# Queries, keys and output gate of a hybrid encoder block as twelve pairs of seven part products

## The chip, the core and the metric

The kernel runs on one core of one Trainium2 chip. The metric is device time in microseconds (us). Three runs of the kernel before gave a median of 2877.66 us (2876.84 to 2880.89).

Five engines work side by side, each in its own program order and held up only by semaphores: TensorE (PE, with its weight loads shown as PEld), VectorE (DVE), ScalarE (ACT), GpSimd (POOL) and SyncE (SP), whose queue issues the DMAs.

## The reference

One encoder block over 2048 tokens of width 1024, in float32:

```python
xn = rms_norm(h, ln_mix_g);  proj = xn @ w_in            # 1024 -> 2512 columns
y_a = mlstm_group(proj q, k, v, o, gates, conv, norm_g)  # 4 heads x 128, both directions
y_b = mla_group(proj c_q, c_kv, k_rope, ...)             # 4 heads, latent queries, keys, values
h = h + concat(y_a, y_b) @ w_out
h = h + conv_gated_mlp(rms_norm(h), w_up, conv, w_down)
h = h + sigmoid(rms_norm(h) @ w_gate) * rms_norm(p @ w_proj)
out = rms_norm(h, final_g)
```

The change concerns `proj` and what follows it directly. Its 2512 columns are queries (512), keys (512), values (512), output gate (512) and a rest of 464 (16 gates, 256 query latents, 128 key-value latents, 64 rotary key columns). Queries and keys go through a depthwise convolution of width 3 along the tokens and a SiLU. Values are used as they are. The output gate goes through a sigmoid and multiplies the normed mLSTM output. The query latents are normed, multiplied by `w_uq`, and 64 columns of every head are rotated.

## The kernel before, in words

**Precision.** Each float32 operand is split into a high and a low part (`split`, L116: ACT casts the high part, DVE subtracts; `split_g`, L125, also multiplies by a gain). A product is three matmuls (`mm3`, L131): low by high, high by low, high by high.

**Stages.** `run` (L150) calls `in_proj`, then `attend` with the mLSTM as a side generator, then `stream`. PSUM has eight banks. During `in_proj` and `attend` they are four of pool `sc` and four of pools `tr`, `pv`, `ml`; during `stream` they are `fx`, `fy`, `fz`, `fs`, two each.

**in_proj (L176).** All of x is split once into sixteen SBUF places `x0` to `x15` and stays there. Three loops over the 16 token tiles follow, each with its weights resident: the rest (`rest`, L253, with the transposes of `turn_rest`, L283, two tiles later), the values (L330 to L338), the output gate (L340 to L348). One tile of one loop is `nat` (L212): 8 blocks of 128 inputs by 3 matmuls. The mLSTM gate arithmetic (`gates`, L641, a generator) is advanced once per tile in the second and third loop. Then queries and keys are computed transposed, channels on partitions: for each of 8 blocks of 128 channels, 4 blocks of 512 tokens, 24 matmuls each (`block`, L385), followed by convolution and SiLU (`taps`, `silu`). Within these blocks a second generator, `side`, is advanced every second input block: `absorb` (L528, it multiplies latent matrices into each other) and `q_up` (L573, the latent queries with their rotation). The last two blocks of channel block 7 stand in the attention.

**attend (L981).** For 64 pairs of head and query tile: scores, exponentials, transposes, the product with the latent values. The mLSTM (`mlstm`, L750) is advanced beside it at a rate set by the constant `SIDE`.

**stream (from L1535).** Output projection, MLP and the last gate. Here a product of 2 by 2 blocks is made from seven part products instead of eight (Strassen's scheme in Winograd's form). A *pair* is two output blocks of 128 by two blocks of 512 tokens; its seven products are called by `prod`, L1472, 12 matmuls each: A11 B11, S1 T1, S2 T2, A12 B21, S3 T3, A22 T4, S4 B22. The last two of a pair run inside the next pair. S1 to S4 are sums of weight blocks, T1 to T4 sums of the other operand. `sum4` (L1231) makes such sums, writes them to DRAM, and `split_op` (L1322) brings them back and splits them into the `x` places.

**Order.** A planner orders the instructions of each engine from their program order and its own estimate of times; in `manual_schedule` blocks the named engine keeps the written order. All DMAs of these stages are issued on SP's queue.

## Time and profile before

| | |
|---|---|
| median of the runs | 2877.66 us |
| profiled execution, its own time | 2877.3 us |
| its span, first to last instruction | 2875.3 us |
| PE busy | 2844.8 us, 99% |
| DVE busy | 2040.0 us, 71% |
| ACT busy | 1503.9 us, 52% |
| POOL busy | 216.6 us, 8% |
| moved by DMA | 508.93 MB, mean 177 GB/s |
| rest loop, value loop, output gate loop | from 7.6 us to 281.9 us of the span |
| queries and keys | from 281.9 us to 492.3 us |
| attention with mLSTM | from 492.3 us to about 1206 us |
| output projection, MLP, last gate | from about 1218 us to the end |

The page's first part gives each engine's busy time, its second the span in 40 slices. A "window" row gives the busy time of each engine between two points of the span with the number of instructions, the clock granted to PE, the share of the DMA engines and GB/s. A "group" row gives line, engine, operation, output and inputs, shape, count, then busy us, mean ns of one, and the idle time before them with what ended it. A "timeline" row gives start, length, engine, line and count of instructions in a row. Matmuls overlap in their pipeline, so that the length of one is more than the distance to the next; distances are read from the starts.

### The profile page before, as it was taken

The numbers are of one execution on the slowest core, as the hardware profiler recorded it, in microseconds if no ns is written. First come the engines' busy times: TensorE is split into PE (matmuls) and PEld (weight loads), VectorE is DVE, ScalarE is ACT, GpSimd is POOL, SyncE is SP. The second block draws the span as 40 slices with busy tenths as digits, with TensorE's granted clock in tenths as the row PEclk, the third lists the DMA queues.
The fourth block names the chain that finished last, engine by engine and source line by source line (L and its number), as shares of the span: only waits on it lengthen the run. The fifth ranks groups of instructions, "written<-read, shape, count | busy, mean of one in ns | idle before, by whom it ended". The sixth has DMA issues, their size and how long they took to land.

```text
span 2875.3 us, 40181 instructions
## 1 busy us (share of the span) xinstructions
PE 2844.8 (99%) x14110; PEld 2389.0 (83%) x14110; DVE 2040.0 (71%) x3726; ACT 1503.9 (52%) x3006; POOL 216.6 (8%) x331
## 2 busy tenths in 40 slices
PE   8999999999999999999999999999999999999998
PEld 7888888888888888888888888888888788888787
DVE  7521565777777777877778877877778767676787
ACT  7311544656666666755655555655556333254665
POOL 3100000000000100034200000000000000011012
PEclk9999999999999999999999999999999999999999
DMA  6612545464443333478845544657776757576864
GB/s 190 133 59 75 165 119 172 126 188 130 132 133 109 102 115 109 142 240 270 273 136 183 192 166 161 208 180 237 237 236 200 239 193 245 167 264 203 283 202 163
DMA packets 408313, 508.93 MB, mean 177 GB/s; under 512 B 34080, under 2 KB 271664, under 8 KB 408112
## 3 DMA queue, kind: packets, MB, share of 16 engines
q1 hardware_dynamic: 408112, 506.37, 55.4%
q8 instruction: 111, 1.82, 0.2%
q14 instruction: 90, 0.74, 0.1%
HBM read 324.16 MB, written 182.12 MB: 176 GB/s over the span
## 4 chain that ended last, share of the span: by engine, by line
PE 51%; DMA 3%; DVE 3%; ACT 1%; issue 1%; POOL 0%; SPq 0%; POOLq 0%; ACTq 0%; DVEq 0%
PE fy L1472 20%; PE fz L1472 14%; PE fx L1472 13%; PE fs L133 1%; DMA opr<-tw_d 1%; DMA opr<-t_d 1%; DVE op L123 1%; DVE fw L123 0%; ACT op L120 0%; DVE fgv L1520 0%; PE fs L1770 0%; PE fs L1894 0%; PE tb L997 0%; PE ppv L1009 0%; ACT fw L120 0%
## 5 line engine op out<-in xcount | busy, mean ns | idle before, releaser
L1472 PE MATMUL fz<-op,fw 128*128 128x512 f32 x1968 | 479.9, 392 | 5.1 <-ACT fw L120 4.8
L1472 PE MATMUL fx<-op,fw 128*128 128x512 f32 x1968 | 475.8, 390 | 0.0
L1472 PE MATMUL fy<-op,fw 128*128 128x512 f32 x1968 | 474.6, 390 | 0.0
L1472 PEld LDWEIGHTS fz<-op,fw 128*128 128x128 f32 x1968 | 368.1, 188 | 84.2 <-ACT fw L120 6.4
L1472 PEld LDWEIGHTS fy<-op,fw 128*128 128x128 f32 x1968 | 368.6, 188 | 76.4
L1472 PEld LDWEIGHTS fx<-op,fw 128*128 128x128 f32 x1968 | 368.1, 188 | 76.0
L120 ACT CAST pt<-tb 128x512 fp32r<-128x512 f32 x256 | 147.4, 586 | 179.9 <-PE tb L997 178.8
L1472 PE MATMUL fy<-op,fwd 128*128 128x512 f32 (+1 forms) x984 | 238.0, 390 | 0.6 <-DVE uv L1457 0.6
L133 PE MATMUL bk<-wsp,xh 128*128 128x512 f32 (+1 forms) x768 | 234.5, 387 | 0.0
L939 DVE TENSOR_REDUCE mx<-bk 128x1 f32<-128x512 f32 x256 | 175.0, 685 | 68.0 <-PE bk L938 66.1
L1472 PEld LDWEIGHTS fy<-op,fwd 128*128 128x128 f32 x984 | 182.7, 188 | 38.5 <-DVE uv L1457 1.0
L123 DVE TENSOR_TENSOR pt<-tb,pt 128x512 fp32r<-128x512 f32 x256 | 173.2, 684 | 33.2 <-ACT pt L120 31.8
L1009 PE MATMUL ppv<-pt,kv 128*128 128x512 f32 x512 | 188.8, 407 | 1.0 <-DVE pt L123 1.0
L956 ACT ACTIVATE pe<-bk,nm 128x512 f32<-128x512 f32 x256 | 174.7, 698 | 16.7 <-DVE nm L950 14.6
L133 PEld LDWEIGHTS bk<-wsp,xh 128*128 128x128 f32 x768 | 145.6, 190 | 25.2
L133 PE MATMUL bk<-wsp,xl 128*128 128x512 f32 (+1 forms) x384 | 150.8, 393 | 7.6 <-DVE xl L123 7.6
L133 PE MATMUL bk<-xh,wqk 128*128 128x512 f32 x480 | 157.1, 393 | 0.0
L997 PE MATMUL tb<-ident,pe 128*128 128x128 f32 x1024 | 150.7, 273 | 3.9 <-DVE pt L123 3.6
L1010 PE MATMUL ppv<-pt,kv 128*128 128x256 f32 x512 | 144.6, 282 | 0.0
L997 PEld LDWEIGHTS tb<-ident,pe 128*128 128x128 f32 x1024 | 121.9, 140 | 24.2 <-DVE pt L123 7.3
L120 ACT CAST fw<-hraw 128x1024 fp32r<-128x1024 f32 (+1 forms) x72 | 70.2, 980 | 116.0 <-PE fx L1472 58.9
L120 ACT CAST op<-opr 128x512 fp32r<-128x512 f32 x165 | 96.2, 620 | 63.3 <-DMA opr<-tw_d 15.0
(365 smaller groups left out, 5161.1 us busy)
## 6 DMA issues: line engine op xcount, KB each, us to landing
fwr<-in_w_up SPq DMA_DIRECT2D x66, 512.0 KB, 5.0
fh<-h_d SPq DMA_DIRECT2D x48, 512.0 KB, 4.0
h_d<-fh SPq DMA_DIRECT2D x48, 512.0 KB, 3.7
s_d<-fwr SPq DMA_DIRECT2D x44, 512.0 KB, 2.6
fws<-s_d SPq DMA_DIRECT2D x44, 512.0 KB, 3.5
rw<-row_d SPq DMA_DIRECT2D x32, 512.0 KB, 5.2
tw_d<-tsum SPq DMA_DIRECT2D x60, 256.0 KB, 5.0
opr<-tw_d SPq DMA_DIRECT2D x60, 256.0 KB, 4.7
```

What stands on the lines that cost most here:

```text
L120: nc.scalar.copy(hi, src)
L123: (sub or nc.vector).tensor_tensor(lo, src, _f(hi), op=ALU.subtract)
L133: mm = lambda *a, **k: self.nc.tensor.matmul(*a, **k, skip_group_check=more)
L939: nc.vector.tensor_reduce(s.mx[:, kb:kb + 1], ps, axis=AX.X, op=ALU.max)
L956: nc.scalar.activation(s.pe[:, kb % 2], s.banks[kb], AF.Exp, bias=s.nm, accum_out=s.rs[:, kb:kb + 1])
L997: nc.tensor.transpose(t[:, j, :], s.p[kb][:, j * P:(j + 1) * P], self.ident)
L1009: mm(w.ps, vh[:, ks], pts[kb][:, j], start=kt == 0, stop=False, skip_group_check=True)
L1010: mm(w.ps[:, 0], vl[:, ks], pts[kb][:, j, 0], start=False, stop=kt == NT - 1, skip_group_check=True)
L1472: nc.tensor.matmul(out, a[:, k * P:(k + 1) * P], parts[lo][:, cols], start=first, stop=lo == 1 and k == last, skip_group_check=more)
```

## The change

Values stay a plain product, but are computed tile by tile together with the rest: `nat` with the rest's weights, then `nat` with the values' weights, for each of the 16 tiles; x is no longer kept but split for each tile into one of two places (`x14`, `x15`). Beside these tiles a generator `work` is advanced three times per tile: `weight_sums` (the sums S1 to S4 of the six pairs of weight blocks, written to DRAM as `sp_d`), then, from tile 8, `token_sums` (norm and gain multiplied into x of the first 1024 tokens, its sums T1 to T4, split or stored as `xo_d`), then `pair_begin`, the first pair's weights.

Then PSUM changes to the pools `fx`, `fy`, `fz`, `fs`, and `pairs` computes queries, keys and output gate as 12 pairs: 6 pairs of channel blocks by 2 blocks of 1024 tokens, seven part products each. The sums of the second token block are made beside pairs 1 to 4 (`sums`) and brought in at pairs 5 and 6 (`load`), the mLSTM gate arithmetic runs beside pairs 7 to 10, the latent matrices and the key latents beside pair 11. The output gate comes out transposed, so the mLSTM multiplies by it after its own transposes (one DVE product in place of an ACT copy), and four scalar products of the norm become one with a broadcast operand.

Then PSUM changes back, and `queries` computes the latent queries in a stage of its own, eight chunks of 256 tokens, with PE in written order; the split of latents and values and the products of `w_out` with the latent value matrices stand between the chunks. The first scores of the attention are in its last two chunks. `SIDE` goes from 668 to 658, and one pause of the mLSTM from 5 steps to 7.

Cut to its core ("+" and "-" as usual; what is left out stands in the words above):

```diff
 SB = 512
 LAG_T, LAG_X, LAG_R = 1, 2, 2
...
-        tail = self.in_proj()
-        self.attend(tail(self.mlstm()))
+        self.in_proj()
+        left.close()
+        pools(left, "left", ("fa", 2))
+        right.close()
+        pools(right, "right", ("fb", 2))
+        self.pairs()
+        left.close()
+        pools(left, "left", ("sc", 4))
+        right.close()
+        pools(right, "right", ("tr", 2), ("pv", 1), ("ml", 1))
+        self.queries()
+        self.attend(self.mlstm())
...
-        ws = load_w(OFF_V, 512)
-        for st in range(NT):
-            ps = nat(st, ws, 512)
...
+        def vals(st):
+            ps = nat(st, wv, 512)
+            t = self.at("t4", [P, 512], name="vo")
             nc.vector.tensor_scalar(t, ps, rcol[:, st:st + 1], None, op0=ALU.mult)
             nc.sync.dma_start(self.v_d[st], t)
-            if st >= LAG_R:
-                next(gates, None)
-
-        ws = load_w(OFF_O, 512)
-        go = self.row_bcast(self.at("t6", [P, 512], name="go"), d["mlstm_norm_g"][0], 512)
-        for st in range(NT):
-            ps = nat(st, ws, 512)
-            t = self.at(next(trot), [P, 512], name="vo")
-            nc.scalar.activation(t, ps, AF.Sigmoid, scale=rcol[:, st:st + 1])
-            nc.vector.tensor_tensor(t, t, go, op=ALU.mult)
-            nc.sync.dma_start(self.o_d[st], t)
-            next(gates, None)
-        for _ in gates:
-            pass
-
...
+        work = self.weight_sums()
+        for st in range(2, NT):
...
+            if st == 8:
+                norm_row(0)
+                work = chain(work, self.token_sums(), self.pair_begin())
+            if st + 2 < NT:
+                load_x(st + 2)
+            if st + 1 < NT:
+                split_x(st + 1)
+                ssq_x(st + 1)
+            ps = nat(st, wr, NREST)
+            rest(st, ps)
+            next(work, None)
+            if st + 1 < NT:
+                rms_x(st + 1)
+            if st == NT - 2:
+                continue
+            if st == NT - 1:
+                vals(st - 1)
+                turn_rest(st - 1)
+            next(work, None)
+            vals(st)
+            turn_rest(st)
+            next(work, None)
+        for _ in work:
+            pass
+        norm_row(1)
+
...
+    def weight_sums(self):
+
+        nc = self.nc
+        tt = nc.vector.tensor_tensor
...
+        nxt = load(0)
+        yield
+        for pr in range(6):
+            g, v = nxt
+            if pr < 5:
+                nxt = load(pr + 1)
+            tt(v[:, hi], v[:, lo], v[:, hi], op=ALU.add)
+            tt(v[:, lo], g[:, lo], v[:, lo], op=ALU.subtract)
+            nc.sync.dma_start(self.sp_d[pr, 0], v)
+            yield
+            tt(g[:, lo], v[:, hi], g[:, lo], op=ALU.subtract)
+            tt(g[:, hi], g[:, hi], g[:, lo], op=ALU.subtract)
+            nc.sync.dma_start(self.sp_d[pr, 1], g)
+            yield
+
...
+        nxt = load(0)
+        yield
+        for k in range(4):
+            a, b = nxt
+            if k < 3:
+                nxt = load(k + 1)
+            for t, kt in ((a, k), (b, k + 4)):
+                nc.vector.scalar_tensor_tensor(t, t, self.gcol[:, kt:kt + 1], rr, op0=ALU.mult, op1=ALU.mult)
+            nc.sync.dma_start(self.xo_d[0, 6, k], b[:, H])
+            yield
+            split("B11", k, a[:, L])
+            tt(a[:, H], a[:, H], a[:, L], op=ALU.subtract)
+            split("T1", k, a[:, H])
+            yield
+            tt(a[:, H], b[:, H], a[:, H], op=ALU.subtract)
+            split("T2", k, a[:, H])
+            tt(a[:, L], a[:, H], a[:, L], op=ALU.subtract)
+            nc.sync.dma_start(self.xo_d[0, 4, k], a[:, L])
+            yield
+            split("B21", k, b[:, L])
+            tt(b[:, L], b[:, L], a[:, H], op=ALU.subtract)
+            nc.sync.dma_start(self.xo_d[0, 5, k], b[:, L])
+            yield
...
+    def pair_load(self, i):
+
+        nc, pr = self.nc, i % 6
+        g = self.at("w12", [P, KT, P], name="fwr")
+        nc.sync.dma_start(g, self.w_tile(pr, 0))
+        v = self.at("w13", [P, 4, P], name="fwr")
+        nc.sync.dma_start(v, self.w_tile(pr, 1, 4))
+        sv, sg = [self.at(t, [P, D], name="fws") for t in ("w0", "w1")]
+        nc.sync.dma_start(sv, self.sp_d[pr, 0])
...
+    def pair_prep(self, i):
+
+        flat = lambda t: t.rearrange("p k c -> p (k c)")
+        g, v, sv, sg = self.raw.pop(i)
+        ops = self.ops[i] = {}
+        ops["A11"], ops["A12"] = self.up_pair(flat(g))
+        yield
+        ops["S3"], ops["S1"] = self.up_pair(sv)
+        yield
+        ops["S2"], ops["S4"] = self.up_pair(sg)
+        yield
+        d = self.at(("w10", "w2")[i % 2], [P, 2, SB], F32R, "fwd")
+        self.split(flat(v), d[:, 0], d[:, 1])
+        ops["A22"] = d[:, 0], d[:, 1]
...
+        def prod(out, w, x, more=False):
+            wh, wl = w
+            ops = self.xop[x]
+            first = not more
+            for a, lo in ((wh, 0), (wl, 0), (wh, 1)):
+                for k, parts in enumerate(ops):
+                    nc.tensor.matmul(out, a[:, k * P:(k + 1) * P], parts[lo], start=first,
+                                     stop=lo == 1 and k == 3, skip_group_check=more)
+                    first = False
...
+        for i in range(12):
...
+            def side(at):
+                if 0 < i < 5:
+                    next(sums, None)
+                if i == 0 and at in (1, 2):
...
+                if gates:
+                    self.gate_bank = prev.spare if at % 2 else s.spare
+                    next(gates, None)
...
+            prod(x, s.ops["A11"], "B11")
+            nc.scalar.copy(s.y, x)
...
+            prod(s.z, s.ops["S1"], "T1")
...
+            if prev:
+                rest_y(prev)
...
+            prod(s.y, s.ops["S2"], "T2", True)
+            s.u[0] = self.at(next(urot), [P, 2 * SB + 2], name="ug")
+            nc.scalar.copy(s.u[0][:, 1 + SB:1 + 2 * SB], s.y)
...
+            if i + 1 < 12:
+                for _ in self.pair_prep(i + 1):
+                    pass
+            if i + 2 < 12:
+                self.pair_load(i + 2)
...
+            prod(x, s.ops["A12"], "B21", True)
+            first_half(s, 0, x)
...
+            if prev:
+                rest_z(prev)
...
+            prod(s.y, s.ops["S3"], "T3", True)
+            s.u[1] = self.at(next(urot), [P, 2 * SB + 2], name="uv")
+            add(s.u[1][:, 1 + SB:1 + 2 * SB], s.p5, s.y)
...
+        rest_y(prev)
+        rest_z(prev)
...
+        def rope(c):
+            t = cc[c]
+            ps = self.gbank([P, 2, NH, 64], "qpr")
+            for e in range(2):
+                ts = slice(e * P, (e + 1) * P)
+                    self.mm3(ps[:, e], t[:, 0, kt, ts], t[:, 1, kt, ts], rw(kt, 0), rw(kt, 1), kt == 0, kt == 1)
...
+            for e in range(2):
+                x1, x2 = ps[:, e, :, 0:32], ps[:, e, :, 32:64]
...
+                for a, b, f, out, op in ((x1, x2, 0, o[:, e, :, 0:32], ALU.subtract), (x2, x1, 1, o[:, e, :, 32:64], ALU.add)):
+                    nc.vector.scalar_tensor_tensor(tt[:, f, 0], a, ASCALE, cos, op0=ALU.mult, op1=ALU.mult)
+                    nc.vector.scalar_tensor_tensor(tt[:, f, 1], b, ASCALE, sin, op0=ALU.mult, op1=ALU.mult)
+                    nc.vector.tensor_tensor(out, tt[:, f, 0], tt[:, f, 1], op=op)
...
+        def turn(c):
+            o = ro.pop(c)
...
+            p2 = self.gbank([P, 2, 2, P])
+            for i in range(2):
+                for e in range(2):
+                    nc.tensor.transpose(p2[:, i, e], o[:, e, 2 * i:2 * i + 2].rearrange("p h e -> p (h e)"), self.ident)
+            flat = p2.rearrange("p i e t -> p i (e t)")
+            self.split(flat, so[:, 0], so[:, 1])
...
+            for c in range(8):
+                rope(c)
+                if c and c < 4:
+                    weights(c)
...
+                if c == 1:
+                    self.vh, self.vl = self.split_latent(2, ("x10", "x11"))
+                if c == 2:
+                    self.kr2, self.krl = self.split_latent(1, ("x14", "x15"))
+                if c + 2 < 8 and c:
+                    split_c(c + 1)
+                if c:
+                    turn(c - 1)
+                latent(c, 0)
+                if c == 6:
+                    split_c(7)
+                latent(c, 1)
+                if c == 4:
+                    att = self.attend_begin()
```

792 lines of the change are left out of this document (439 added, 353 removed).

## The prediction

> **What bounds the kernel now.** I read the page's first two parts first, then windows by stage, then the groups of PE kept apart by shape, then PE's timeline for the distance between matmuls, and last who PE waited for.
>
> ```profile
> PE 2844.8 (99%) x14110; PEld 2389.0 (83%) x14110; DVE 2040.0 (71%) x3726; ACT 1503.9 (52%) x3006; POOL 216.6 (8%) x331
> ```
>
> PE is never without work for long. The windows say that this holds stage by stage, and how full DVE and the DMA are beside it (columns: stretch, its length, busy us of PE, PEld, DVE, ACT, POOL with counts, clock, DMA share, GB/s):
>
> ```profile
> 190.00:281.90 91.90, 91.90 (x407) 76.10 (x406) 17.69 (x31) 18.04 (x30) 0.00 (x0) 1.00 0.16 59
> 281.90:492.30 210.40, 210.40 (x1082) 178.61 (x1081) 121.91 (x311) 94.28 (x183) 0.00 (x0) 1.00 0.52 158
> 1300.00:1430.00 130.00, 129.71 (x616) 107.10 (x616) 94.83 (x128) 79.67 (x159) 52.99 (x52) 1.00 0.88 279
> 1429.37:1753.05 323.68, 323.68 (x1430) 268.02 (x1429) 250.65 (x309) 172.02 (x238) 0.00 (x0) 1.00 0.49 167
> 1753.05:1829.61 76.56, 76.44 (x338) 62.97 (x337) 65.97 (x84) 54.57 (x83) 0.00 (x0) 1.00 0.64 212
> 2690.00:2700.00 10.00, 7.52 (x26) 5.44 (x25) 9.65 (x14) 5.71 (x9) 0.00 (x0) 0.83 0.81 267
> ```
>
> Output gate, then queries and keys: PE without a gap, DVE at 19% and 58%. The MLP's pairs of seven part products: PE full with DVE at 77%, and a change of operands (fifth row) hardly shows. The last row is the warning: PE waited once, and the clock granted in these 10 us is 0.83. So a wait is charged twice.
>
> A busy matmul is not the price of a matmul. PE's timeline:
>
> ```profile
> 1445.45 2.88 PE L1472 MATMUL fy<-op,fwd 128*128 128x512 f32 x12
> 1448.17 2.88 PE L1472 MATMUL fy<-op,fw 128*128 128x512 f32 x12
> 1464.49 2.88 PE L1472 MATMUL fy<-op,fwd 128*128 128x512 f32 x12
> 46.28 0.50 PE L240 MATMUL ssp<-ones,x_ss 128*128 128x4 f32 x4
> 52.15 0.50 PE L240 MATMUL ssp<-ones,x_ss 128*128 128x4 f32 x4
> 327.53 1.60 PE L133 MATMUL gb<-cq,wq 128*128 128x256 f32 x12
> 328.96 0.40 PE L133 MATMUL bk<-xh,wqk 128*128 128x512 f32 x1
> 2695.26 3.35 PE L1472 MATMUL fz<-op,fw 128*128 128x512 f32 x8 [2.42 <-ACT fw L120]
> ```
>
> Twelve matmuls of 512 columns start 2.72 us after the twelve before, so 0.2267 us each; a pair of 84 takes 1464.49 - 1445.45 = 19.04 us. A whole tile of the rest takes 52.15 - 46.28 = 5.87 us, a tile of values 24 x 0.2267 = 5.44 us, and twelve matmuls of 256 columns 1.43 us.
>
> **The change part by part.** *1. Matmuls removed.* The groups of the four products by shape:
>
> ```profile
> L133 PE MATMUL bk<-wsp,xh 128*128 128x512 f32 x512 | 157.9, 390 | 0.0
> L133 PE MATMUL bk<-wsp,xl 128*128 128x512 f32 x256 | 100.7, 393 | 0.0
> L133 PE MATMUL bk<-xh,wqk 128*128 128x512 f32 x480 | 157.1, 393 | 0.0
> L133 PE MATMUL bk<-xl,wqk 128*128 128x512 f32 x240 | 93.9, 391 | 0.0
> L133 PE MATMUL gb<-xh,wqk 128*128 128x512 f32 x32 | 10.3, 392 | 0.0
> L133 PE MATMUL gb<-xl,wqk 128*128 128x512 f32 x16 | 6.2, 389 | 0.0
> ```
>
> Values and output gate have 512 + 256 = 768, so the gate alone 384; queries and keys have 480 + 240 + 32 + 16 = 768. That is 1152. Twelve pairs of 84 are 1008, and pairs 0 and 1 have one extra matmul each: 142 fewer. At 0.2267 us this is **-32.2 us**; at the mean length of 390 ns it would be 55, but lengths overlap. All other PE work (rest, values, latent queries, transposes) keeps its count. The Trainium skill ("TensorE: Matmul & The Clock Gate", Back-to-back issue gap) gives about 131 ns for a sustained 512-column matmul with its weight load and 216 ns for an isolated one; estimated from that page, the saving would be 18.6 or 30.7 us. The trace's distance lies above both, and decides.
>
> What is left is what PE has to wait for in the new stages. Durations on DVE:
>
> ```profile
> L123 DVE TENSOR_TENSOR xl<-x_t,xh 128x512 fp32r<-128x512 f32 x32 | 21.1, 684 | 0.8 <-ACT xh L120 0.7
> L123 DVE TENSOR_TENSOR woa<-wor,woa 128x1024 fp32r<-128x1024 f32 x4 | 4.9, 1223 | 1.6 <-ACT woa L120 1.6
> L129 DVE SCALAR_TENSOR_TENSOR wsp<-wraw,gcol,wsp 128x512 fp32r<-128x512 f32 x16 | 11.3, 748 | 0.7 <-ACT wsp L128 0.7
> L234 DVE TENSOR_TENSOR x_ss<-x_ss 128x256 f32<-128x256 f32 x16 | 6.7, 417 | 0.0
> L257 DVE SCALAR_TENSOR_TENSOR gt<-bk,rcol,bg 128x8 f32<-128x8 f32 x32 | 5.9, 226 | 4.9 <-PE bk L133 4.4 <-POOL rcol L245 0.4
> L270 DVE SCALAR_TENSOR_TENSOR nn<-rs,rsr,gn 128x256 f32<-128x256 f32 x16 | 7.8, 486 | 18.6 <-POOL rsr L143 18.6
> L271 DVE SCALAR_TENSOR_TENSOR nn<-rs,rsr,gn 128x128 f32<-128x128 f32 x16 | 5.5, 347 | 0.0
> L274 DVE TENSOR_TENSOR sc<-rs,sc 128x32 f32<-128x32 f32 x16 | 3.1, 195 | 1.4 <-ACT rs L260 0.6
> L335 DVE TENSOR_SCALAR vo<-bk,rcol 128x512 f32<-128x512 f32 x16 | 12.0, 750 | 40.3 <-PE bk L133 40.3
> L613 DVE SCALAR_TENSOR_TENSOR qtt<-qpr,qcs 128x128 f32<-128x128 f32 x16 | 4.6, 285 | 3.3 <-PE qpr L133 3.2
> L123 DVE TENSOR_TENSOR wq<-wqr,wq 128x768 fp32r<-128x768 f32 x2 | 1.9, 959 | 2.4 <-DMA wo_d<-woo 2.2
> L1520 DVE SCALAR_TENSOR_TENSOR fgv<-ug,fcw,fgv 128x1024 f32<-128x1024 f32 x34 | 43.5, 1279 | 0.0
> L1427 DVE TENSOR_TENSOR fwr<-fwr 128x512 f32<-128x512 f32 x17 | 11.8, 692 | 0.6
> ```
>
> *2. The start: +3 us (0 to 7).* After two tiles of the rest the first tile of values needs the values' weights split: eight DVE operations of 0.75 us, 6 us, behind the split of tile 1 (1.22), two sums of squares (0.69 + 0.42 each) and the work of tile 0 (about 2.6). Together some 12 us, while PE has 2 x 5.87 = 11.7 us of work; the tile then follows the splits. Nothing lost if the planner puts the splits first; 7 us if all of them stand behind.
>
> *3. The tiles: +2 us (0 to 14).* PE needs 5.87 + 5.44 = 11.3 us per tile. DVE: split 1.22, squares 1.11, gates 0.45, latents 0.49 + 0.35, seven small ones of 0.19, values 0.75: 5.7 us. Three steps of the weight sums add 6 x 0.69 = 4.2 (9.9 in all); three steps of the token sums 3/4 of (2 x 1.28 + 4 x 0.69 + 4 x 0.68) = 6.0 (11.7 in all, for 5 2/3 tiles). So DVE falls behind by some 2 us there, and x is split a tile ahead, which hides it. The upper end is the DMA, a rival below.
>
> *4. Two changes of PSUM pools: +2 us (0 to 6).* Each bank is waited for by itself, and the first pair's operands are made beside the tiles; at the second change two splits of 0.96 us and a chunk's 0.68 precede the first rotation, while PE has the 24 matmuls that end the last pair and six of `w_out`. The one wait of 2.42 us above, at a like place, is the row nearest to it; with the slow clock after it each change costs at most about 3.
>
> *5. The pairs: +1 us (0 to 4).* DVE per pair: splits 3 x 1.22 + 0.68, two additions of 0.69, two convolutions of 2 x 1.28: 10.8 us. The sums of the second block add 4 x 0.75 + 4 x 0.69 = 5.8: 16.6 of 19.04 us, 87%. Bringing in the second block takes 28 x 0.68 = 19 us of DVE over pairs 5 and 6, which follow output gate pairs without convolution. The nearest row, the MLP's own change of operands, is four pairs in 76.56 us against 4 x 19.04 = 76.16: 0.4 us. The gate arithmetic beside pairs 7 and 8 is hidden by DVE's remaining 8 us per pair; without that cover it would cost as much as it is long.
>
> *6. The latent queries: +6 us (1 to 15).* They stood within the 210 us of queries and keys with DVE at 58%, and now stand alone. PE per chunk: 36 matmuls at 1.43 / 12 = 0.119 and four transposes, 4.7 us. DVE per chunk: split 0.68, twelve rotations of 0.285, split 0.68: 4.8 us. The stage: PE 8 x 4.7 + 24 x 0.2267 + 20 scores x 0.2267 = 47.6 us; DVE 8 x 4.8 + 2 x 0.96 + 3 x (1.22 + 0.29) + 8 x 0.68 = 50.3 us, of which chunks 1 and 2 have 9 us each against 6.1 on PE. DVE is the longer by 2.7 us; with PE in written order every handover adds some, and I take half a us per chunk. The lower end is DVE running ahead during the last pair, where it has no convolution and no next pair to split.
>
> *7. The attention: -1 us (-4 to 3).* It loses two query and key blocks (counted in 1) and their convolutions; the mLSTM changes four scalar products for one and moves a 512-wide copy from ACT to DVE. DVE is at 77% there, and 99% of PE stays.
>
> Sum: -32.2 + 3 + 2 + 2 + 1 + 6 - 1 = -19.2 us. From the profiled execution's own 2877.3 us (0.4 below the median) this gives **2858 us**.
>
> **The rivals.** *Nothing is lost.* The planner left no wait worth naming in most stages, and where DVE is at 77% PE is full. Then only 0 to 1 us per term is paid, and the attention gains a little: 2877.3 - 32.2 = 2845. Against it: DVE above 85% in three places.
>
> *The DMA holds up the tiles.* The weight sums load and store six times 2.1 MB = 12.6 MB within 4 1/3 tiles or 49 us, beside 1.15 MB per tile of x, values and latents: 17.6 MB, 359 GB/s. The most that a stretch above shows is 279, at a DMA share of 0.88. At 279 the work takes 63 us, 14 us more; DVE, in order, waits at a sum whose blocks have not come, and the split of the next x stands behind it. For it speaks the rate; against it that five steps after the sums are empty and x is split a tile ahead. If it decides, 14 instead of 2: 2870 us.
>
> *The latent queries go one after another, and the kernel is slower.* If a chunk's rotation, split and transposes do not overlap the next chunk's, it takes 1.43 + 4.8 + 3.3 = 9.5 us instead of 4.7: +38 us over eight chunks, and a clock that falls after waits adds to it: 2877.3 - 32.2 + 7 + 38 = 2890 us. It decides from 25 us, 3.1 us per chunk. For it: written order on PE, one buffer each for products and result of the rotation. Against it: 2.86 us of latent products and the transposes of the chunk before stand between two rotations.
>
> The fall of the clock is in the trace: after the wait of 2.42 us, eight matmuls take 3.35 us, and 10 us at 0.83 are 1.7 us lost. The Trainium skill (same page, Part 1: The HAM clock gate) says that an idle window of about 3.4 us halves the clock until about 3.4 us of work; the trace agrees on the half clock, though a wait of 2.42 us was enough.
>
> **How the numbers follow.** The forecast, 2849 to 2866: 0.60. Nothing lost: 0.15. The DMA, 2866 to 2876: 0.15, of which 0.05 lies within 0.2% of the time before. Slower through the latent queries: 0.10, of which 0.01 within 0.2%. 0.2%, 5.8 us, is about what a measurement of this kernel can tell from no change. So faster 0.84, within 0.2% 0.06, slower 0.10. The range leaves out the lower part of the second case and the last one: 2846 to 2876. The ends of all terms together would reach from 2842 to beyond the time before.
>
> **What would show it.** Right: 1008 matmuls of `prod`'s line in the new stage and 384 fewer of the output gate, pairs 19.04 us apart, PE's idle before the pairs 4 to 8 us above today's, DVE near 90% in the tiles, and the latent stage near 54 us with PE waiting for a split of a chunk or its rotation. Wrong: a DMA of the weight sums as the end of waits in the tiles with a share of 0.9; chunks 8 us or more apart; a granted clock below 1 over a whole stage; pairs further apart than 20 us, which would mean that DVE has become the bound.

## The result and the profile after

The changed kernel takes **2890.04 us** (median of 5 runs, 2886.02 to 2894.39) against 2876.85 us before (5 runs, 2876.67 to 2880.89): a ratio of 1.0043, 95% interval 1.0028 to 1.0058. It is slower by 0.4%; 2858 was forecast, with a range to 2876.

The profiled execution took 2890.04 us itself, its span is 2887.9. The page after:

```profile
span 2887.9 us, 40258 instructions
PE 2822.1 (98%) x13970; PEld 2364.1 (82%) x13970; DVE 2138.3 (74%) x3751; ACT 1577.4 (55%) x3037; POOL 213.0 (7%) x331
```

There are 14110 - 13970 = 140 fewer matmuls, and the groups of `prod`'s line hold 3 x 288 + 144 = 1008:

```profile
L545 PE MATMUL fy<-op,fw 128*128 128x512 f32 x288 | 70.2, 391 | 0.0
L545 PE MATMUL fz<-op,fw 128*128 128x512 f32 x288 | 69.8, 390 | 1.5 <-DVE ug L511 1.0 <-DVE fw L125 0.5
L545 PE MATMUL fx<-op,fw 128*128 128x512 f32 x288 | 69.4, 390 | 0.0
L545 PE MATMUL fy<-op,fwd 128*128 128x512 f32 x144 | 37.5, 411 | 9.2 <-DVE uv L511 5.1 <-DVE uv L563 4.1
```

The work was removed as counted; the last group, A22 T4, is the one that PE waits for most. The windows by stage (tiles, pairs, latent queries up to the first score, the attention's entry) show that PE was no longer full beside it:

```profile
0.00:202.50 202.50, 188.15 (x899) 158.89 (x900) 138.48 (x355) 90.63 (x170) 35.09 (x70) 1.00 0.75 234
202.50:446.80 244.30, 233.66 (x1028) 190.42 (x1026) 168.47 (x289) 159.18 (x220) 0.00 (x0) 0.99 0.77 242
446.80:501.70 54.90, 45.49 (x314) 41.69 (x313) 33.47 (x108) 26.83 (x47) 0.00 (x0) 0.94 0.76 227
501.70:530.00 28.30, 23.99 (x141) 19.80 (x141) 18.44 (x45) 14.55 (x32) 0.00 (x0) 1.00 0.73 212
```

To see what each stage lost I worked out its **excess**: the time between the starts of its first matmul and the next stage's (of the last stage, its last matmul's), less its matmuls at their usual distance (0.2267 us at 512 columns, 0.208 at 464, 0.114 at 256, about 0.11 at 128). It holds the waits and the slow clock behind them, and some error of the distances: the 288 latent products of 256 columns come every 0.120 us in both kernels, so 1.7 us of the latent queries' excess after are no wait. In us:

| stage | before | after |
|---|---|---|
| up to the first pair (before: tiles and output gate) | 5.0 | 13.5 |
| pairs (before: queries, keys and latent queries) | 3.5 | 17.0 |
| latent queries up to the first score | - | 13.5 |
| first 29 us from the first score | 0.2 | 5.9 |
| rest of the attention | 27.0 | 30.1 |
| all behind it | 14.1 | 14.3 |
| sum | 49.8 | 94.3 |
| all matmuls at their usual distance | 2808.0 | 2776.0 |

So 32.0 us of matmul time went and 44.5 us of excess came; the spans differ by 2887.9 - 2875.3 = 12.6. Whom PE waited for, first in the tiles (the wait of 7.6 us is the start's, there before too), then from the pairs to the entry (us in all, times, longest):

```profile
PE bk L135 <- DVE xh L125: 7.6, 1, 7.6
PE rtp L290 <- DVE nn L274: 3.6, 6, 1.5
PE rtp L290 <- DVE nn L284: 2.7, 4, 1.6
```

```profile
PE fy L545 <- DVE uv L511: 5.1, 3, 2.6
PE gb L135 <- DVE qtt L837: 5.0, 3, 1.7
PE fy L545 <- DVE uv L563: 4.1, 3, 2.8
PE qpr L135 <- ACT woo L819: 3.2, 1, 3.2
PE bk L1200 <- ACT pe L1222: 2.3, 1, 2.3
PE qpr L135 <- DVE nm L1216: 1.5, 1, 1.5
```

Four causes are to be seen in the timeline. The first, in the pairs: the sum that makes `uv` (L511) has its operands, but stands in DVE's queue behind a tap of the convolution (at 241.35, not shown), a product for the second block's sums, the other tap and a weight split. Its product's bank is to be filled further by A22 T4, the third product of the next pair, and PE waits for it:

```profile
242.61 0.74 DVE L608 SCALAR_TENSOR_TENSOR tsum<-tsum,gcol,rrow 128x512 f32<-128x512 f32 x1
243.27 1.28 DVE L567 SCALAR_TENSOR_TENSOR ct<-ug,fcw,ct 128x1024 f32<-128x1024 f32 x1
244.47 1.22 DVE L125 TENSOR_TENSOR fw<-fwr,fw 128x1024 fp32r<-128x1024 f32 x1
245.67 0.68 DVE L511 TENSOR_TENSOR uv<-p,fy 128x512 f32<-128x512 f32 x1
246.40 0.96 PE L545 MATMUL fy<-op,fwd 128*128 128x512 f32 x3 [2.81 <-DVE uv L563]
```

The second, behind the output gate's pairs: `uv` is to be written into a place from which the gate of the pair before is still being stored. With three `u` places in turn, `uv` of a pair always has the place of the `ug` before it (in the first cause too, so that `uv` there can't go ahead of the taps, which read that place):

```profile
322.43 0.37 SPq L577 DMA_DIRECT2D o_d<-ug  x1
329.29 0.69 DVE L511 TENSOR_TENSOR uv<-p,fy 128x512 f32<-128x512 f32 x1 [2.62 <-DMA o_d<-ug]
```

The third, at the first chunk of latent queries: ScalarE's copy `woo` goes to u2, from which the last gate is being stored; its bank stays taken, PE waits for it, and from 459.8 to 466.6 us the granted clock is 0.50:

```profile
455.33 0.42 SPq L577 DMA_DIRECT2D o_d<-uv  x1
459.80 0.58 ACT L819 COPY woo<-gb 128x512 f32<-128x512 f32 x1 [1.37 <-DMA o_d<-uv]
460.43 0.80 PE L135 MATMUL qpr<-wq,cq 128*128 128x256 f32 x2 [3.15 <-ACT woo L819]
```

```profile
459.80:466.60 6.80, 6.17 (x22) 5.25 (x22) 0.88 (x4) 1.75 (x3) 0.00 (x0) 0.50 0.40 137
```

The fourth, in the chunks 1 to 3: two more banks are taken there for `w_out`, so the rotation of four gives the first latent product the bank of the same chunk's rope product, which DVE still reads (1.7 us three times). The later chunks, without `w_out`, come every 4.75 us, and PE waits for nothing there:

```profile
487.52 1.60 PE L135 MATMUL qpr<-wq,cq 128*128 128x256 f32 x12
492.27 1.60 PE L135 MATMUL qpr<-wq,cq 128*128 128x256 f32 x12
```

### The profile page after: what moved, and what is told of

The parts are those of the page before. It is cut to its first block, busy times and chain, and to the rows that moved or that the text cites. A ratio compares the mean times of both kernels' runs of the same rounds, so it can differ in the third digit from the quotient of the medians.

```text
span 2887.9 us, 40258 instructions
## 1 busy us (share of the span) xinstructions
PE 2822.1 (98%) x13970; PEld 2364.1 (82%) x13970; DVE 2138.3 (74%) x3751; ACT 1577.4 (55%) x3037; POOL 213.0 (7%) x331
## 4 chain that ended last, share of the span: by engine, by line
PE 77%; DMA 8%; DVE 6%; ACT 4%; issue 3%; POOL 1%; SPq 1%; POOLq 0%; ACTq 0%; DVEq 0%
PE fy L1736 21%; PE fz L1736 14%; PE fx L1736 14%; PE ppv L1275 3%; PE tb L1263 3%; PE bk L135 2%; PE bk L1203 2%; PE bk L1200 2%; PE bk L1204 2%; PE bk L1201 2%; PE bk L1202 2%; PE ppv L1276 2%; PE fs L135 1%; PE fy L545 1%; DMA fwr<-in_w_in 1%
## 5 line engine op out<-in xcount | busy, mean ns | idle before, releaser
L125 DVE TENSOR_TENSOR op<-opr,op 128x512 fp32r<-128x512 f32 x205 | 134.0, 690 | 34.2 <-ACT op L122 34.2
L122 ACT CAST op<-opr 128x512 fp32r<-128x512 f32 x205 | 119.8, 620 | 71.4 <-DMA opr<-tw_d 16.5
L125 DVE TENSOR_TENSOR fw<-fwr,fw 128x1024 fp32r<-128x1024 f32 x100 | 122.0, 1220 | 24.3 <-ACT fw L122 24.3
L1784 DVE SCALAR_TENSOR_TENSOR fgv<-uv,fcw,fgv 128x1024 f32<-128x1024 f32 x88 | 112.8, 1282 | 16.9 <-ACT fgv L1782 16.2
L122 ACT CAST fw<-fwr 128x1024 fp32r<-128x1024 f32 x100 | 105.0, 1051 | 36.4 <-DVE fwr L1710 21.6
```

The lines of the kernel that those rows point to most:

```text
L122: nc.scalar.copy(hi, src)
L125: (sub or nc.vector).tensor_tensor(lo, src, _f(hi), op=ALU.subtract)
L1784: nc.vector.scalar_tensor_tensor(t, u[:, tap:tap + 2 * SB], self.taps[:, tap, ct:ct + 1], t, op0=ALU.mult, op1=ALU.add)
```

## The experiments

Every kernel is an edit of the changed one; times are compared with the kernel before on the same chip. This table is used in all that follows: median, ratio to the kernel before with its interval where there is one, and the excess up to the first pair, in the first 115 us of pairs (pairs 0 to 5), in the other pairs, in the latent queries, and in the entry. Each cell is one profiled execution. How far a cell can be trusted is told by the part behind the attention, which no edit touches: 10.1 to 17.0 us over the same profiles. The twelve kernels with the tiles unedited span 12.0 to 15.5 us in that column. The kernel before took 2875.2 to 2875.8 us in the experiments' measurements and 2876.85 beside the changed kernel, so by the ratios a gain over the changed kernel is 1 to 2 us smaller than by the medians.

| kernel | us | ratio | tiles | pairs 0-5 | pairs 6-11 | latent | entry |
|---|---|---|---|---|---|---|---|
| changed | 2890.0 | 1.0043 (1.0028-1.0058) | 13.5 | 7.5 | 9.5 | 13.5 | 5.9 |
| a_woo | 2884.2 | 1.0028 (1.0017-1.0039) | 12.0 | 6.1 | 11.0 | 7.5 | 6.7 |
| b_wbank | 2883.9 | 1.0029 (1.0019-1.0040) | 15.3 | 7.6 | 11.3 | 4.0 | 5.3 |
| c_ogate | 2884.6 | 1.0034 (1.0021-1.0047) | 13.9 | 8.9 | 7.0 | 10.8 | 6.7 |
| d_fewer_stores | 2886.1 | 1.0039 (1.0025-1.0053) | 14.4 | 6.0 | 9.9 | 10.3 | 6.7 |
| p_u_order | 2883.8 | 1.0027 (1.0015-1.0038) | 12.8 | 6.5 | 7.9 | 11.6 | 6.9 |
| m_no_sums | 2883.4 | one run | 13.9 | 0.5 | 11.4 | 12.0 | 5.6 |
| n_pool_sums | 2898.3 | 1.0082 (1.0065-1.0099) | 15.5 | 16.8 | 11.3 | 11.9 | 5.5 |
| e_lag | 2888.6 | 1.0044 (1.0029-1.0059) | 11.9 | 9.9 | 8.5 | 10.4 | 7.5 |
| f_wsum_stores | 2892.0 | one run | 10.8 | 8.2 | 12.1 | 10.3 | 7.3 |
| h_early | 2885.9 | 1.0040 (1.0025-1.0055) | 13.5 | 8.3 | 10.9 | 12.4 | 3.6 |
| r1_three | 2885.1 | 1.0032 (1.0019-1.0045) | 14.9 | 14.3 | 7.3 | 6.1 | 5.6 |
| r2_five | 2885.3 | 1.0032 (1.0021-1.0043) | 15.9 | 13.5 | 5.4 | 8.4 | 5.3 |
| x1_uorder_lag | 2875.1 | 0.9999 (0.9990-1.0009) | 11.9 | 3.6 | 4.6 | 8.4 | 3.6 |
| x2_own_places | 2882.2 | 1.0018 (1.0008-1.0028) | 13.6 | 7.2 | 4.6 | 11.2 | 5.2 |
| x3_sums_spread | 2876.4 | 1.0001 (0.9992-1.0011) | 13.3 | 6.6 | 5.9 | 8.7 | 5.2 |
| y1_no_catch_up | 2873.9 | 0.9993 (0.9984-1.0002) | 14.7 | 5.3 | 5.1 | 7.0 | 5.6 |
| y2_krope_later | 2875.1 | 0.9995 (0.9986-1.0004) | 12.5 | 4.7 | 7.8 | 5.7 | 7.3 |
| y3_two_cosines | 2873.8 | 0.9994 (0.9985-1.0003) | 13.3 | 3.7 | 7.8 | 5.8 | 5.7 |

The single edits' intervals overlap with that of the changed kernel, but for n_pool_sums; what the others show lies in the stage and in the rows of waits, not in the totals.

**The latent queries: a place and a bank.**

```diff
-                o = self.at(("t6", "t7")[hf] if False else ("t6", "u2")[hf], [P, 512], name="woo")
+                o = self.at(("t6", "t7")[hf] if False else ("t6", "t4")[hf], [P, 512], name="woo")
```

> Edit to the changed kernel alone: the second half of a head's output weight product is written to t4 instead of u2. Theory 1 (a place still in use): ScalarE waits at 457 us for the store of the last output gate out of u2, and the PE waits 3.2 us behind it and then has half its clock for 6.8 us. With t4, whose keys are read for the last time earlier, the group 'PE qpr L135 <- ACT woo' is gone, and no half clock follows at 460 us: 5 to 7 us less than the changed kernel, about 2884. Theory 2 (the stage is late anyway: its first rope products wait for the split of the first chunk or of the weights): the wait stays with another name behind it, and the time moves by under 1.5 us.

```diff
-                ps = self.gbank()          # weights(h)
+                ps = self.bank()
```

> Edit to the changed kernel alone: the two output weight products of a head take their PSUM banks from the four score banks, which stand empty until the attention, not from the rotation of the four others. Theory 1 (the rotation): with two more banks taken per chunk, the first latent product of chunks 1, 2 and 3 is given the bank of the same chunk's rope product, which DVE still reads; 'PE gb L135 <- DVE qtt L837: 5.0, 3' goes to nothing and the time falls by 4 to 5 us, to about 2885. Theory 2 (DVE is the bound of these chunks, as my third rival had it): the latent queries then wait for a later split or rope product; the chunks 1 to 3 keep their spacing within 0.5 us each, and the time moves by under 1.5 us.

Both fell to their first theory: the latent queries lose 7.5 and 4.0 us instead of 13.5, and the totals are 6 us lower (4 by the ratios). With the other place the row for `woo` is gone and the clock is 1.00 from 451 to 494 us; the rope's row stays. With the other banks the group 'gb <- qtt' is gone, and `woo` has a bank to spare and delays nothing; one wait of 2.0 us stays. PE's waits in these two kernels:

```profile
PE gb L135 <- DVE qtt L837: 5.2, 3, 1.9
```

```profile
PE qpr L135 <- DVE qtt L837: 2.0, 1, 2.0
```

**The pairs: places, stores or DVE.**

```diff
-                t = u[:, 1:1 + 2 * SB]
-                nc.scalar.activation(t, t, AF.Copy, scale=go[:, h:h + 1])
+                t = self.at(("x10", "x11")[half], [P, 2 * SB], name="ot")
+                nc.scalar.activation(t, u[:, 1:1 + 2 * SB], AF.Copy, scale=go[:, h:h + 1])
```

> Edit to the changed kernel alone: the four output gate pairs write their gate to x10 and x11, which nothing uses in this stage, and store it from there; the three u places are free as soon as ScalarE has read them. Theory 1 (places): the rows 'DVE uv L511 <- DMA o_d<-ug' and what the PE waits behind them (5.1 us in 3 waits for uv L511, and the half clock of 3.4 us at 330 us) go; 4 to 8 us less, 2882 to 2886; the wait for woo stays or shrinks too, since the last gate no longer leaves from u2: then 8 to 13 us less, 2877 to 2882. Theory 2 (DMA bandwidth): the stores come late because the queues are full with the second block's sums, whatever place they leave from; the wait moves to the next load or sum, under 3 us less.

```diff
-                    if i != 1:
-                        nc.sync.dma_start(self.xo_d[1, (0, 0, 3, 6)[i], k], t[i])
...
-                nc.sync.dma_start(raw, self.xo_d[blk, self.NAMES.index(n), k])
+                nc.sync.dma_start(raw, self.xo_d[0, 4 + self.NAMES.index(n) % 3, k])
```

> Left out: the stores of the second block's seven sums in pairs 1 to 4 (28 stores of 256 KB, 7.3 MB); the second block then loads stored operands of the first, so its output is not the layer's; all sums are still computed on DVE. Theory 1 (DMA bandwidth holds up the pairs): DMA falls from 285 to 297 GB/s to about 200 in the pairs 1 to 4, the waits for tsum loads and for the gate store in the pairs 4 to 6 go, and the excess of the pairs over their matmuls (15 us) falls below 5: 2878 to 2882. Theory 2 (places and the order on DVE): the excess stays over 10 us and the time within 4 us of the changed kernel, 2886 to 2892.

```diff
-        rot, urot = _rot("t", range(4)), _rot("u", range(3))
+        rot, urot = _rot("t", range(4)), itertools.cycle(("u2", "u0", "u1", "u0"))
```

> Edit to the changed kernel alone: the same three u places, handed out in another order: the second half of each pair (uv) always has u0, the first half (ug) u2 and u1 in turn. Theory 1 (places): with three places in turn, uv of pair i is written over ug of pair i-1, so its sum, which frees the bank for the next product, has to wait on DVE for both taps of that convolution and for the store of that gate; in the new order it waits for neither. The rows 'PE fy L545 <- DVE uv L511' and '<- DVE uv L563' (9 us together) shrink to under 3, 'DVE uv L511 <- DMA o_d' goes, and since u2 no longer holds the last gate, 'PE qpr <- ACT woo' goes too: excess of pairs 1 to 6 from 15 us to under 7, 10 to 16 us less in all, 2874 to 2880. Theory 2 (DVE is simply full: 16.4 us of work in a pair of 20.5 us, in order): another wait takes the place, the excess of the pairs stays over 11 us; only the woo part goes, 5 to 7 us less.

```diff
-                    nc.vector.scalar_tensor_tensor(t[i], t[i], self.gcol[:, kt:kt + 1], rr[i % 2], ...)
...
-                tt(t[1], t[1], t[0], op=ALU.subtract)
```

> Left out: all arithmetic of the second block's seven sums in the pairs 1 to 4 (32 DVE instructions, some 23 us of DVE); their loads and stores stay, with unsummed contents. Theory 1 (places): the second half's sum still has to come behind the convolution of the first half before it; the wait at 243 us (2.8 us) shrinks, since DVE is ahead, but the wait at 327 us behind the gate's store stays. Theory 2 (DVE is full): all waits before 320 us go, about 7 us less than the changed kernel. Both see no change behind 380 us.

Bandwidth is refuted as the cause: with 7.3 MB fewer stores the DMA falls from 280 to 233 GB/s between 202 and 340 us, and the pairs still lose 15.9 us. And without the sums' arithmetic (one run) the same transfers go at 297 GB/s while PE has no gap. The first 115 us of pairs, first of the changed kernel, then of m_no_sums:

```profile
202.50:317.50 115.00, 109.33 (x478) 88.54 (x476) 82.71 (x126) 68.56 (x94) 0.00 (x0) 1.00 0.88 280
202.90:317.90 115.00, 115.00 (x509) 94.76 (x506) 68.44 (x105) 75.83 (x104) 0.00 (x0) 1.00 0.93 297
```

So PE's waits in the pairs 0 to 5 end on DVE's queue, and they come with the sums in it. That edit also takes away DVE's own waits for the blocks that it sums (5.9 us); in d_fewer_stores these are 2.1 us and 6.0 us are still lost, so they are the smaller part. Places alone do not explain these pairs: the other order of places takes the waits for `uv` from 9.2 to 1.3 us, but those for `ug` grow from 1.0 to 3.9, and 6.5 of 7.5 us remain:

```profile
PE fz L545 <- DVE ug L511: 3.9, 3, 2.6
PE fy L545 <- DVE uv L511: 1.3, 2, 1.1
```

They have a share in it, though, which one execution doesn't show: the four later kernels with this order and the sums unchanged (x1, y1, y2, y3) lose 3.6 to 5.3 us there, the nine without it and with the sums on DVE 6.0 to 9.9.

In m_no_sums a wait of 2.7 us behind the gate's store stays, as the theory of places said; places of their own for the gates or the other order remove it. In the pairs 6 to 11 all kernels with either edit lose 4.6 to 7.9 us, all others 8.5 to 12.1. So DVE's queue with the sums in it decides in the pairs 1 to 4, with places for some 3 us of it, and places decide behind them. Neither edit gave the time that the theory of places forecast: c_ogate took 5.4 us off instead of 8 to 13, p_u_order 6.2 instead of 10 to 16. The wait for `woo` went in both, but those for DVE's `qtt` in the latent queries grew from 5.0 to 6.4 and 7.2 us, and in c_ogate 3.9 us of waits for ScalarE came into the pairs.

```diff
-                tt(t[1], t[1], t[0], op=ALU.subtract)            # and three more per k
+                nc.gpsimd.tensor_tensor(t[1], t[1], t[0], op=ALU.subtract)
```

> Edit to the changed kernel alone: the four subtractions of the second block's sums (16 instructions, 0.69 us each on DVE, 11 us in all) are computed on GpSimd, which has nothing to do in the pairs. Theory 1 (DVE's queue is what the PE waits for in the pairs 1 to 4): with a fifth of its work there gone, the excess between the first pair and 317 us falls from 7.5 to 2 or 3 us, and the wait at 243 us goes; the one behind the gate's store at 327 us stays; 4 to 6 us less, 2884 to 2886. Theory 2 (GpSimd takes several us for one and slows DVE beside it): the sums come later, the loads of the second block's operands with them, and the pairs 5 and 6 lose more than the pairs 1 to 4 gain: 2890 or more.

Slower by 8 us than the changed kernel (11 by the ratios), and most of it in the pairs 0 to 5, which lose 16.8 us instead of 7.5. The second theory had the time and the slower DVE right, but looked for the loss in the pairs 5 and 6. The groups of DVE by shape between 202 and 320 us, first of the changed kernel, then of this one:

```profile
L608 DVE SCALAR_TENSOR_TENSOR tsum<-tsum,gcol,rrow 128x512 f32<-128x512 f32 x16 | 11.8, 747 | 5.9 <-DMA tsum<-in_x_turned 5.9
L567 DVE SCALAR_TENSOR_TENSOR ct<-ug,fcw,ct 128x1024 f32<-128x1024 f32 x8 | 10.2, 1279 | 0.0
```

```profile
L608 DVE SCALAR_TENSOR_TENSOR tsum<-tsum,gcol,rrow 128x512 f32<-128x512 f32 x16 | 15.9, 1002 | 6.1 <-DMA tsum<-in_x_turned 6.1
L567 DVE SCALAR_TENSOR_TENSOR ct<-ug,fcw,ct 128x1024 f32<-128x1024 f32 x8 | 14.2, 1777 | 0.1
```

DVE's own operations grow by 34 and 39%: in these two groups alone 8 of the 11 us that were taken off it come back, and a subtraction takes GpSimd 1.4 to 2.2 us against 0.69 on DVE. Its timeline:

```profile
244.12 1.70 DVE L125 TENSOR_TENSOR fw<-fws,fw 128x1024 fp32r<-128x1024 f32 x1
244.81 2.14 POOL L617 TENSOR_TENSOR tsum<-tsum 128x512 f32<-128x512 f32 x1
245.80 1.70 DVE L608 SCALAR_TENSOR_TENSOR tsum<-tsum,gcol,rrow 128x512 f32<-128x512 f32 x1
```

The Trainium skill ("SBUF — State Buffer", SBUF: two separate sides) says that a DVE operation with two SBUF inputs and a GpSimd operation that reads SBUF take turns at one pair of ports, each for its whole length. The trace agrees: the same DVE operations take 1.70 us beside GpSimd that take 1.22 and 0.75 without it.

A slower DVE is not all of it. GpSimd's four subtractions end at 235.4 us, the loads of the next four blocks are issued from 236.26 us instead of 232.62, and DVE stands 5.49 us at the first; the `ug` that PE wants is behind it, and PE waits 3.89 us. How the 16.8 us divide between the two was not measured:

```profile
239.93 0.75 DVE L608 SCALAR_TENSOR_TENSOR tsum<-tsum,gcol,rrow 128x512 f32<-128x512 f32 x1 [5.49 <-DMA tsum<-in_x_turned]
```

**The tiles.**

```diff
             if st == NT - 2:
+                turn_rest(st - 1)
                 continue
...
             vals(st)
-            turn_rest(st)
+            if st == NT - 1:
+                turn_rest(st)
+            elif st > 2:
+                turn_rest(st - 1)
```

> Edit to the changed kernel alone: from the third tile on, a tile's latents are turned behind the values of the next tile and not of their own (a lag of one tile more, as the kernel before had it). Theory 1 (the chain): 'PE rtp L290 <- DVE nn' (6.3 us in 10 waits) goes to under 1 and the excess of the tiles falls from 13.5 to 6 or 8 us: 2883 to 2886. Theory 2 (DMA: DVE stands at the weight sums and the split of the next tile's x is late as well): the waits move to the first products of the next tile, under 2.5 us less.

```diff
-            nc.sync.dma_start(self.sp_d[pr, 0], v)
+            if not pr:
+                nc.sync.dma_start(self.sp_d[0, 0], v)
...
-        nc.sync.dma_start(sv, self.sp_d[pr, 0])
+        nc.sync.dma_start(sv, self.sp_d[0, 0])
```

> Left out: ten of the twelve stores of weight sums (5.2 of 12.6 MB, in the tiles 2 to 7); every pair then loads the sums of the first, so the output is not the layer's. Theory 2 (DMA holds up the tiles, my second rival): DVE's waits for the weight blocks (L407, 11.0 us in 5) fall below 4 and the PE's waits for nn with them; the excess of the tiles falls from 13.5 to about 8. Theory 1 (the chain from rest to turn alone): DVE's waits fall but the PE keeps its 6 us of waits for nn; the excess stays over 11.

Neither theory alone. With the lag, 'rtp <- nn' goes, as the chain would have it, but 5.2 us come back for the sum of squares of the next tile, as the DMA theory had it; the tiles keep 11.9 us:

```profile
PE ssp L244 <- DVE x_ss L239: 5.2, 3, 3.2
```

With ten stores fewer, DVE's waits for weight blocks fall from 12.4 only to 8.4 us, PE's for `nn` from 6.3 to 4.8, and the tiles lose 10.8 us (one run), a little under the 12.0 to 15.5 us of the kernels with unedited tiles. Both point to DVE's queue, though no edit shows it: whatever DVE stands at, the work behind it is late for PE, be it a turn or the next x. DVE's longest waits in the tiles, 19.5 us in 13 for GpSimd's `rsr` (16.8 in 14 before), were left alone. What the remaining 10 us of the tiles are is not settled.

**The entry.** `next(att)` for the scores at the fifth chunk instead of the sixth.

> Edit to the changed kernel alone: the first scores of the attention stand behind the fifth chunk of latent queries and not behind the sixth, so that two chunks (9.5 us) lie between them and the next tile's scores. Theory 1 (ScalarE's exponentials have one chunk's time and need more): 'PE bk L1200 <- ACT pe L1222' (2.3 us) goes, the excess of the attention's entry falls from 5.9 to 3 or less: 3 to 4 us less. Theory 2 (the order only moves the wait: the split of the last chunk needs the place of the first query tile, and now waits for the scores earlier): within 2 us of the changed kernel.

The wait for ScalarE's exponential is gone and the entry falls from 5.9 to 3.6 us, as the first theory had it; the total, 4 us lower (1 by the ratios), lies within the spread. In kernels with the score banks the gain turns into a wait for the split of the first queries (`bk <- q_s`, 2.5 us and more), and the last three kernels do without it.

**Do the parts add up?**

> Three edits to the changed kernel together: output weight products in the score banks, u places in the order u2, u0, u1, u0, and the subtractions of the sums on GpSimd. If what was seen one by one adds up (latent queries 9 us, pairs 1 to 4 5 us, the pairs behind 3 us): 2871 to 2875, level with the kernel before or up to 5 us ahead. If the waits only change place, as in the u order alone, where 9 us of waits went and 8.5 us came back under other names: 2878 to 2882, still slower than before.

> The three edits and two more: two steps of weight sums in a tile instead of three, so that their 12.6 MB have half as long again, and the first scores behind the fifth chunk. If both help: 3 to 5 us less in the tiles (the waits of DVE for weight blocks, 11.0 us, fall below 4) and 3 less at the attention's entry, so 2864 to 2870, faster than before by 0.2 to 0.4%. If the tiles' loss is the chain from a tile's latents to their turn, the tiles stay at 13 us of excess and the total is within 3 us of the three edits.

No: both carry the subtractions on GpSimd, and the pairs 0 to 5 lose 14.3 and 13.5 us. Two steps of weight sums per tile instead of three did not help either; DVE's waits for weight blocks rose from 12.4 to 18.3 us, for a reason that was not looked into. Without GpSimd:

> Four edits to the changed kernel: output weight products in the score banks, u places u2, u0, u1, u0, first scores behind the fifth chunk, and a lag of one tile more between latents and turn in the tiles 3 to 7 (where the weight sums run). If the losses add up as they showed one by one (latent queries 9 us less, pairs 2, entry 2, tiles 3): excess about 79 instead of 95 us and 2872 to 2876, level with the kernel before. If DVE's load makes a new wait for each: 2880 or more.

> Three edits to the changed kernel: output weight products in the score banks, the gates in places of their own (x10, x11), first scores behind the fifth chunk. DVE's work in the pairs 1 to 4 is as in the changed kernel. If the losses add up (latent queries 8 us less, pairs 2, entry 2): 2877 to 2879; the excess of the first six pairs stays at 7 to 8 us, and the kernel does not come below the one before, since tiles and pairs hold the rest. If not: 2882 or more.

> Score banks, u places u2, u0, u1, u0 and the first scores behind the fifth chunk as in the first of these; besides, the second block's sums have places of their own (x10, x11) and begin in pair 0, so that DVE's 23 us of sums lie in five pairs and not in four. Theory DVE's queue: the excess of the pairs 0 to 5 falls from 7.5 to 3 or less, and the total to 2869 to 2874, below the kernel before. Rival: pair 0 has its own 12 operand loads, and the 16 blocks for the sums come on top of 263 GB/s; the sums come late and stand before other work on DVE, so the pairs keep 7 us or more: 2876 to 2880.

The first of these, level with the kernel before, came as adding up had it: 17 us of excess less, and 15 us of time (13 by the ratios), with intervals that don't touch. The second did not: 2882.2 us where adding up gave 2877 to 2879. Gates in places of their own leave 7.2 us in the pairs 0 to 5, as forecast, but the latent queries lose 11.2 us, with a wait of 4.1 us for the split of the first queries that the changed kernel doesn't have. So part of what an edit takes away comes back elsewhere, and how much depends on the set. Spreading the sums over five pairs left 6.6 us in the pairs 0 to 5, so its rival held.

> Score banks, u places u2, u0, u1, u0 and the lag of the turns in the tiles 3 to 7 as in the run before that came level; the eighth tile's turn now stands ahead of the ninth tile's values, so that two turns don't meet in one bank (3.2 us at 116.7 us), and the first scores stand behind the sixth chunk as in the changed kernel (there the wait for the first queries' split cost 2.5 us and its half clock). If the rows are worth what they show: 4 to 6 us less than that run's 2875.1, 2869 to 2871, faster than before by 0.1 to 0.2%. If new waits take their place: 2874 to 2878.

> As the one before it in this call, and two edits in the latent queries: the rope's cosines of successive chunks in two places (s2, t4), and the split of the rope keys one chunk later. DVE's wait for them (4.0 us) and the PE's wait behind DVE's rope at the fourth chunk (2.3 us) go: 2 to 4 us less than that run; or, if DVE's load is what is late, the wait moves by a chunk and the time within 1 us.

> As the first of this call, with the cosines in two places alone (the rope keys' split stays). If the wait for the cosines' load alone is what holds DVE: 2 to 3 us less than the first; if it is DVE's load in the third chunk, within 1 us of it.

All three end at 2874 to 2875, 0.9993 to 0.9995 of the kernel before with intervals that hold 1: no measurable gain over it, but 15 to 16 us under the changed kernel (14 by the ratios). The 4 to 6 us that y1's rows promised over x1 did not come: it is 1.3 us under it, and its waits took other places. Their pairs still lose 10 to 13 us, the tiles 12 to 15. The two edits of the latent queries take at most 1.3 us off that stage's excess; the gains of 2 to 4 us that they were to bring did not come, and the totals are within the spread of y1's. Of the 44.5 us of new excess x1 and the last three met 12 to 17, between a quarter and two fifths; whether the rest can be met was not tried.

## Why the prediction was wrong

The sum had -32.2 us of matmuls and +13 us for everything else; -32.0 and +44.5 came. The mechanism of the gain was right, and the prices of the new waits were wrong, in the pairs above all.

*1, the matmuls: right.* 1008 of `prod`'s line, and 32.0 us less at the usual distances against 32.2. 140 matmuls fewer and not 142, because two transposes of the rows' norms (L303) are new.

*2 and 3, start and tiles: +5 forecast, +8.5 came.* Within their bounds (0 to 21). The reason was seen too narrowly: x is split a tile ahead, but the turn of a tile's latents follows its own values at once, and `nn` stands on DVE behind a weight sum whose blocks have not come. So my second rival had a part of the mechanism (276 GB/s at 0.87 of the queues between 65 and 100 us, and 12.4 us of DVE's waits for weight blocks), and its size was not what decided.

*5, the pairs: +1 (0 to 4) forecast, and with step 4 (+2) the step that failed most.* Pairs and pool changes together lost 17.0 us; with the latent queries 30.5, where the stage before lost 3.5 and steps 4 to 6 had forecast 9 more. The load was nearly right: 14.0 to 16.5 us of DVE per pair with sums, against 16.6 counted. The inference was wrong, that 87% hides itself because the MLP's pairs run full at 77 and 86%. A share says nothing on order: the sum that frees PE's bank has a deadline of two products, 5.4 us, and sums, taps and a weight split of 0.7 to 1.3 us each stand in front of it. Without the sums 0.5 us are lost, with them on GpSimd 16.8. And no place was looked up: that `uv` takes over the place of the `ug` before it is read from the rotation of three. In the pairs 6 to 11, where the second block's operands come in, PE loses 9.5 us and not 0.4; but the longest waits there, 4.6 us in two with a half clock behind the first, are for a place from which a gate is stored, not for the operands.

*6, the latent queries: +6 (1 to 15) forecast, 13.5 came.* Within the bounds, but for another reason, so that the bounds held by luck. DVE is at 33.47 of 54.90 us where I had counted 50.3, in part because successive rotations start 0.20 us apart, though each is 0.28 long, the same overlap that I had allowed for PE alone. Up to the first score PE waits for nothing in the chunks without `w_out`; the handovers for which I took half a us per chunk cost nothing. What cost was a place (3.2 us, and 3.4 lost in 6.8 us at half the clock) and a bank rotation (3 x 1.7); 1.7 us are the products' distance and no loss.

*7, the attention: -1 (-4 to 3) forecast, +8.8 came, outside the bounds.* 5.7 of it at the entry, where the written order leaves one chunk between the first tile's scores and the next tile's, and the exponentials take longer; with one chunk more (h_early) 2.3 us of it go. The other 3.1 us were not traced.

*The rivals.* The third gave 2890 and the sign, but by chance and not by its mechanism: chunks are 4.75 us apart, not 9.5. Of the signs against me named ahead, a stage's clock below 1 came (0.94 in the latent queries), and pairs further apart than 20 us (up to 24.5 between the starts of two pairs' A22 products, in the pairs 0 to 6). The chances, by their parts, add up to 0.85 for faster and 0.09 for slower, not 0.84 and 0.10.

## What to carry to other kernels

A new stage is not priced by shares of busy time. For each operation that frees a bank or a place for PE, write down when PE wants it and what stands ahead of it on its in-order engine, a DMA's landing among it; and for each place and bank that a rotation gives out, who had it last and until when. Here four such lines would have shown some 20 us that no sum of durations did: an estimate from the rows above, 9.2 + 5.0 + 3.2 us of waits and 5.1 us at half the clock. Finding them is not yet gaining them: x1, with edits against all four causes and two more, met 17 us, and a wait that was taken away often came back under another name.

## What the runs showed of the hardware

Work moved from DVE to an idle GpSimd made DVE slower: taps 1279 to 1777 ns, products 747 to 1002 ns; the kernel became 8 us slower, in part because GpSimd's sums came late. And a wait of 3.15 us went with 6.8 us at a clock of 0.50 (from 459.8 us, 0.6 us before its end), twice as long as after the wait of 2.6 us at 329 us, where eight matmuls show it:

```profile
330.10:333.50 3.40, 3.40 (x8) 2.71 (x9) 2.03 (x4) 3.15 (x6) 0.00 (x0) 0.50 0.72 211
```

Why the longer stretch lasts was not looked into. The Trainium skill ("TensorE: Matmul & The Clock Gate", Part 1: The HAM clock gate) names windows of about 3.4 us of idleness and of work. The lengths of 3.4 and 6.8 us agree with one and two such windows; that waits of 2.4 to 3.2 us suffice does not agree with a full window of idleness.
